# Moving the last two-operand GpSimd steps to VectorE and building a 32x32 inverse from blocks of 16 in a two-layer decoder trunk

## The chip, the cores and the metric

The kernel runs on one core of a Trainium2 chip. Its engines are TensorE (PE, matrix products, with its weight loads shown apart as PEld), VectorE (DVE), ScalarE (ACT), GpSimd (POOL) and SyncE (SP, which here issues every DMA). Each engine has a queue of its own and works it off in order. The metric is device microseconds for one execution; lower is better.

## What is computed

Two layers are applied to a sequence of 1024 tokens of width 1024, with a memory cross-attention beside each mixer and a SiLU gate on both. Layer 0 is latent attention with 12 heads, layer 1 a recurrent mixer with 24 heads of width 64:

```python
for i in range(DEPTH):                       # 0: attention, 1: recurrent
    h = rmsnorm(x, norm_g[i])
    u = h @ w_in[i]
    mix = mla_mixer(...) if i == 0 else rwkv7_mixer(...)
    y = concat([mix, memory_attention(...)]) * silu(gate)
    x = x + y @ w_out[i]
return rmsnorm(x, final_g)

def step(state, inp):                        # one token of rwkv7_scan, per head
    r_t, w_t, k_t, v_t, kk_t, a_t = inp
    sa = einsum('bhvk,bhk->bhv', state, -kk_t)
    state = (state * w_t[:, :, None, :] + sa[..., None] * (kk_t * a_t)[:, :, None, :]
             + v_t[..., None] * k_t[:, :, None, :])
    return state, einsum('bhvk,bhk->bhv', state, r_t)
```

All data are float32.

## The kernel before

**Precision and weights.** A float32 product is made of three TensorE products of halves: `split` writes a high part (ScalarE, fp32r) and a low part (a subtraction), and `mm3` (L162 to L164) multiplies high by high, low by high and high by low. `weights` (L142) loads weight tiles of 128x512 from DRAM (tile `wr`, four buffers), lets ScalarE write `wh` and a second engine the low part `wl` (four buffers each). In layer 1 that engine is VectorE (`self.lows`, set at L941). In layer 0 it is GpSimd, save for every second tile of the memory projections. `rope` (L516) multiplies one of its two products on GpSimd (L523), and `project` of the attention layer subtracts the low halves of the rotated queries there (L640, L641).

**Layer 1 in stages.** The 12 head pairs of the recurrent mixer and the two halves of the sequence (512 tokens each) make 24 items. Each item goes through five stages: `project`, `prep`, `invert`, `scan`, `norm`. In step s, item s is projected, item s-1 prepared, item s-2 inverted, and so on, so 28 steps cover all. Within a step the stages are generators, and `interleave` runs them in turns given by `ST = (4, 18, 13, 11, 11)`; between them lie parts of the output projections and of the memory heads. The framework takes that order as a priority and plans every engine's queue from it with costs of its own, so that instructions of all stages mix finely in each queue.

**The recurrence in chunks of 64 tokens.** An item has 8 chunks and 2 heads, so 16 systems of 64x64, unit triangular with a strictly triangular part N. `prep` computes them into `AM` (L1088, L1090), masked. The inverse of such a system is what `scan` multiplies with (`XT`, L1221). It is made of two 32x32 diagonal blocks and one block off the diagonal:

- End of `prep` (L1098 to L1110): the 32 diagonal blocks of 32x32 are written to DRAM (`sysd`, 16 DMAs), and ScalarE copies the off-diagonal parts into `A21`, the first 32 partitions of the tile `inv`.
- Start of `invert`: one DMA reads all blocks into `As`, each four times, one block per partition: partition = (block, column mod 4), free size 32x32. A constant is loaded into `U`.
- The loop of L1134 to L1143: back substitution, for u = 31 down to 1, one product and one sum on VectorE over u rows and up to 8 columns, 62 instructions per item.
- L1147 to L1155: eight TensorE transposes in two groups, evicted by ScalarE, put the columns back into matrices (`Uc`, partitions 32 to 95 of `inv`).
- The tail: a VectorE transpose (`X1`, L1159), copies into `U2` and `XT` (L1161, L1168), a product with `A21` (L1174), ScalarE copies (`M1`, L1183), a second product (L1188) and the copies into `XT` (L1191).

**Scan.** For each of the 8 chunks: `c` (L1215, L1217), a masking product on VectorE (`gm`, L1219), the product with the inverse (L1221), a copy (`SAV`, L1222), the new state (L1224, L1236). Each chunk needs the state of the one before it. `XT` has two buffers, so an item may be inverted while the one before it is scanned.

Of the kernel before, what the change touches and what calls it, by code (L numbers as in the profile page):

```python
# [23 lines left out]
P = 128  # L24
# [47 lines left out]
class Build:  # L72
    def __init__(self, tc, A, st):
        self.tc, self.nc, self.A = tc, tc.nc, A
        self.n, self.lows = 0, False
# [66 lines left out]
    def weights(self, src, cols=1024, shared=False):  # L142

# [3 lines left out]
        for c in range(0, cols, T):  # L147
# [6 lines left out]
            sub = nc.vector.tensor_sub if self.lows or shared and len(res) % 2 else nc.gpsimd.tensor_sub  # L154
            sub(lo[:, :n], raw[:, :n], hi[:, :n].bitcast(F32))  # L155
# [107 lines left out]
    def mem_kv(self, l, ms):  # L263
# [3 lines left out]
        for h in range(4):  # L267
            if h % 2 == 0:
                mk.append(self.g([P, 2, 256], s="mk"))
            w = self.weights(A["wmk"][l, h], shared=True)  # L270
            ps = self.mmt()
            self.gemm(ps[:, :256], w, ms, 8)
            nc.scalar.copy(mk[-1][:, h % 2, :], ps[:, :256])
        for cb in range(2):
            ws = self.weights(A["wmv"][l, cb, 0], shared=True) + self.weights(A["wmv"][l, cb, 1], shared=True)
# [138 lines left out]
    def layer0(self, ahead):  # L414

        nc, A, tc = self.nc, self.A, self.tc
        with ExitStack() as st:
# [98 lines left out]
            def rope(q, hf):  # L516
# [6 lines left out]
                nc.gpsimd.tensor_mul(sw[:], sw[:], sin[:, sl])  # L523
# [84 lines left out]
            def project(h):  # L608
# [26 lines left out]
                for t in rot:  # L635
# [4 lines left out]
                    nc.gpsimd.tensor_sub(a[64:128, :], t[0:64, :], a[0:64, :].bitcast(F32))  # L640
                    nc.gpsimd.tensor_sub(b[0:64, :], t[64:128, :], b[64:128, :].bitcast(F32))  # L641
# [137 lines left out]
    def layer1(self, x1, first, second):  # L779

        nc, A, tc = self.nc, self.A, self.tc
        with ExitStack() as st:
# [19 lines left out]

            cen = tl([P, P], F32, "cen")
# [4 lines left out]
            for t in ARs + XTs + [U2]:  # L808
                nc.gpsimd.memset(t[:], 0.0)
# [3 lines left out]
            env = dict(rmask=rmask, cen=cen, am=am, ip=ip, a_tile=a_tile, b_tile=b_tile, c_tile=c_tile, y_tile=y_tile)  # L813
# [127 lines left out]
            self.lows = True  # L941
# [37 lines left out]
    def prep(self, d, env):  # L979
# [117 lines left out]

        sysd = self.dram.tile([2, 16, 32, 32], F32, tag=f"sys{p % 2}", name=self.name("sysd"))  # L1098
        inv = self.g([P, 16, 32], s="inv")
        A21 = inv[0:32]  # L1100
        for b in range(2):
            for i in range(4):
                src = AM[i][32 * b : 32 * b + 32, :, 0:128].rearrange("p c (h t) -> p c h t", h=2)
                dst = sysd[b, 4 * i : 4 * i + 4].rearrange("(c h) r t -> r c h t", h=2)
                for c in range(2):
                    nc.sync.dma_start(dst[:, c], src[:, c, :, 32 * b : 32 * b + 32])
# [3 lines left out]
        d.update(f=f, SAV=SAV, BKT=BKT, AM=AM, bonus=bonus, inv=inv, sysd=sysd)  # L1110

    def invert(self, d, env):

        XT, U2, inv, sysd = (d[x] for x in ("XT", "U2", "inv", "sysd"))
# [5 lines left out]
        As = ip.tile([P, 32, 32], F32, tag="As", name=self.name("As"))  # L1120
        nc.sync.dma_start(
            As[:].rearrange("p a b -> p (a b)"),
            sysd[:].rearrange("b s r t -> (b s) (r t)").unsqueeze(1).broadcast_to([32, 4, 1024]),
        )
        U = ip.tile([P, 32, 8], F32, tag="U", name=self.name("U"))
        tmp = ip.tile([P, 32, 8], F32, tag="tmp", name=self.name("tmp"))
        E = V
        if d["hf"] == 1:
            c0 = self.smp.tile([P, P], F32, tag="c0", bufs=2, name=self.name("c0"))
            nc.sync.dma_start(c0[:], self.carry[d["p"]][:])  # L1130
            ACT.activation(c0[:], c0[:], AF.Copy, scale=d["f"][:, 8:9])
            d["c0"] = c0[:]
        nc.sync.dma_start(U[:].rearrange("p a b -> p (a b)"), self.A["cst"][:, CU : CU + 256])
        for u in range(31, 0, -1):  # L1134
            if u % 4 == 0:
                yield
            i0 = u // 4
            n = 8 - i0
            E.tensor_tensor(  # L1139
# [239 lines left out]
```

## Time and profile before

| what | us |
|---|---|
| median of 3 runs | 2541.62 (2540.92 to 2550.03) |
| profiled execution, own time | 2544.33 |
| profiled execution, span of the core | 2542.6 |

The page gives busy time by engine and by group of instructions; a group is named by its line, its engine, the tile written and the tiles read, with its shape, count, busy time and mean duration of one in ns. The chain of work that ended last goes back from the last instruction to what released each step. Matmuls overlap and their ends are modelled, so the duration of a matmul is longer than the time it holds the engine; the distance between two starts is what it costs. Layer 0 lasts to about 1080 us of the span, the pipelined steps of layer 1 to about 2445 us, and the rest is the end of the last output projection and the final norm.

### The profile page before, as it was taken

What the parts mean: (1) busy time and instruction counts of PE and PEld (TensorE: products, weight loads), DVE (VectorE), ACT (ScalarE), POOL (GpSimd) and SP (SyncE); (2) the same over time, 40 slices, a digit from 0 to 9 for tenths busy, and PEclk for the clock granted to TensorE, in tenths of its full rate; (3) what the DMA queues carried; (4) which work ended last, traced back from release to release, by engine and by line L of the source; (5) the groups of instructions that cost most, each with busy time, mean ns of one, the idle gap of its engine ahead of it and who ended that gap; (6) DMA issues with size and microseconds to landing.
All of it is one profiled execution on the core that took longest, in us unless ns stands there. A gap on an engine that the chain in (4) does not pass through costs nothing.

```text
span 2542.6 us, 39928 instructions
## 1 busy us (share of the span) xinstructions
PE 2434.1 (96%) x13298; PEld 2003.9 (79%) x13298; DVE 1883.6 (74%) x5564; ACT 1371.9 (54%) x2971; POOL 285.0 (11%) x344
## 2 busy tenths in 40 slices
PE   7899999999999999999999999999999999999997
PEld 5688777888888787878777777877787777788885
DVE  6655433677777647679888888788888888786986
ACT  5444335555445434556566665666666665654542
POOL 3332222322222240000000000000000000000000
PEclk8899999999999999999999999999999999999998
DMA  4242222111111345331222222322222223232341
GB/s 155 88 157 96 91 83 80 50 50 60 55 54 56 135 140 178 122 106 61 80 67 70 74 83 82 120 76 76 69 78 74 75 80 102 92 105 97 115 141 69
DMA packets 165983, 231.46 MB, mean 91 GB/s; under 512 B 46096, under 2 KB 67984, under 8 KB 165776
## 3 DMA queue, kind: packets, MB, share of 16 engines
q1 hardware_dynamic: 165776, 228.90, 27.5%
q8 instruction: 105, 1.72, 0.3%
q14 instruction: 102, 0.84, 0.1%
HBM read 187.66 MB, written 37.49 MB: 89 GB/s over the span
## 4 chain that ended last, share of the span: by engine, by line
PE 69%; DVE 16%; ACT 6%; issue 3%; DMA 2%; SPq 0%; DVEq 0%; POOL 0%; ACTq 0%; POOLq 0%
PE mm L162 14%; PE mm L163 13%; PE mm L164 13%; PE a L1088 3%; DVE tmp L1139 2%; PE c L1221 2%; PE pt L726 2%; DVE U L1143 2%; PE c L1224 1%; PE po L162 1%; PE y L1228 1%; PE po L163 1%; DVE wl L155 1%; PE y L1227 1%; PE po L164 1%
## 5 line engine op out<-in xcount | busy, mean ns | idle before, releaser
L153 ACT CAST wh<-wr 128x512 fp32r<-128x512 f32 (+3 forms) x500 | 298.6, 599 | 461.6 <-PE mm L163 363.0
L162 PE MATMUL mm<-xnh,wh 128*128 128x512 f32 x912 | 374.1, 411 | 0.8 <-DVE qml L134 0.6
L163 PE MATMUL mm<-xnl,wh 128*128 128x512 f32 x912 | 371.4, 407 | 0.0
L164 PE MATMUL mm<-xnh,wl 128*128 128x512 f32 x912 | 369.8, 406 | 0.0
L155 DVE TENSOR_TENSOR wl<-wr,wh 128x512 fp32r<-128x512 f32 (+2 forms) x352 | 237.2, 676 | 98.7 <-ACT wh L153 79.8
L155 POOL TENSOR_TENSOR wl<-wr,wh 128x512 fp32r<-128x512 f32 (+1 forms) x148 | 186.3, 1263 | 579.4 <-ACT wh L153 446.0
L162 PE MATMUL mm<-yh,wh 128*128 128x512 f32 x492 | 199.8, 406 | 5.5 <-DVE xr L391 5.3
L164 PE MATMUL mm<-yh,wl 128*128 128x512 f32 x492 | 197.6, 402 | 0.0
L162 PEld LDWEIGHTS mm<-xnh,wh 128*128 128x128 f32 x912 | 172.2, 189 | 30.4 <-issue 2.6
L163 PE MATMUL mm<-yl,wh 128*128 128x512 f32 x492 | 196.1, 399 | 0.0
L163 PEld LDWEIGHTS mm<-xnl,wh 128*128 128x128 f32 x912 | 172.4, 189 | 27.2 <-issue 1.4
L164 PEld LDWEIGHTS mm<-xnh,wl 128*128 128x128 f32 x912 | 172.2, 189 | 27.2 <-issue 1.0
L1069 POOL MEMSET SAV<- 64x512 f32 x48 | 24.9, 524 | 1385.6 <-DVE m L1261 250.7
L162 PE MATMUL mm<-xh,wh 128*128 128x512 f32 x416 | 168.9, 406 | 7.2 <-ACT xh L440 7.2
L163 PE MATMUL mm<-xl,wh 128*128 128x512 f32 x416 | 168.6, 405 | 2.9 <-DVE xl L441 2.9
L164 PE MATMUL mm<-xh,wl 128*128 128x512 f32 x416 | 168.1, 404 | 0.0
L1139 DVE TENSOR_TENSOR tmp<-As,U 128x60 f32<-128x60 f32 (+24 forms) x744 | 156.8, 211 | 13.2 <-DMA U<-in_cst_dram 1.1
L1143 DVE TENSOR_TENSOR U<-U,tmp 128x60 f32<-128x60 f32 (+24 forms) x744 | 157.2, 211 | 11.9
L1235 ACT ACTIVATE sc<-S,f 128x128 f32<-128x128 f32 x168 | 67.4, 401 | 170.0 <-DVE S L1236 155.5
L304 ACT ACTIVATE p<-b,sm 128x512 f32<-128x512 f32 (+2 forms) x144 | 82.9, 579 | 117.2 <-DVE sm L301 78.0
L391 DVE TENSOR_TENSOR xr<-mm,xr 128x512 f32<-128x512 f32 x123 | 84.5, 689 | 77.7 <-PE mm L164 77.2
L162 PEld LDWEIGHTS mm<-yh,wh 128*128 128x128 f32 x492 | 93.1, 189 | 24.3 <-DVE xr L391 3.5
(362 smaller groups left out, 6214.3 us busy)
## 6 DMA issues: line engine op xcount, KB each, us to landing
wr<-in_wu_dram SPq DMA_DIRECT2D x292, 256.0 KB, 2.6
wr<-in_wo_dram SPq DMA_DIRECT2D x122, 256.0 KB, 2.6
yr<-y SPq DMA_DIRECT2D x60, 256.0 KB, 3.7
As<-sysd SPq DMA_DIRECT2D x24, 512.0 KB, 4.3
y<-y SPq DMA_DIRECT2D x32, 256.0 KB, 2.0
y<-sg SPq DMA_DIRECT2D x32, 256.0 KB, 2.0
g<-u SPq DMA_DIRECT2D x24, 256.0 KB, 2.4
gt<-g SPq DMA_DIRECT2D x24, 256.0 KB, 2.8
```

Source lines behind the costliest of these rows:

```text
L153: nc.scalar.copy(hi[:, :n], raw[:, :n])
L155: sub(lo[:, :n], raw[:, :n], hi[:, :n].bitcast(F32))
L162: mm(ps, a[0], b[0], start=start, stop=False)
L163: mm(ps, a[0], b[1], start=False, stop=False)
L164: mm(ps, a[1], b[0], start=False, stop=stop)
L304: nc.scalar.activation(p[:, :own], ps[:, :own], AF.Exp, bias=sm[:, 0:1], accum_out=sm[:, 2 + i : 3 + i])
L391: nc.vector.tensor_add(xs[m][:], ps[:], xs[m][:])
L726: nc.tensor.transpose(pt[:, o : o + P], src, self.ident)
L1088: mm(ps[:, j * 256 : j * 256 + 256], BK[c // 4][:, c % 4, :], AR[:, c, :], start=True, stop=True)
L1139: E.tensor_tensor(out=tmp[:, 0:u, 0:n], in0=As[:, 0:u, u : u + 1].broadcast_to([P, u, n]), in1=U[:, u : u + 1, i0:8].broadcast_to([P, u, n ...
L1143: E.tensor_tensor(out=U[:, 0:u, i0:8], in0=U[:, 0:u, i0:8], in1=tmp[:, 0:u, 0:n], op=ALU.add)
L1235: ACT.activation(sc[:], cur, AF.Copy, scale=fc)
```

## The change

The change has two parts.

**GpSimd to VectorE.** `weights` always subtracts on VectorE; the product in `rope` and the two subtractions of the rotated queries move to VectorE. GpSimd keeps its memsets.

**The inverse from blocks of 16.** `prep` writes each 64x64 system whole (8 DMAs) and no longer fills `A21`. `invert` reads the four 16x16 diagonal blocks of each of the 16 systems, each twice, into `As` (8 DMAs of 16 partitions; partition = (column half, block, system)), and `A21` by a DMA. The substitution runs over u = 15 down to 1 with 8 columns each, so 30 instructions. ScalarE makes a transposed copy `UT`. Both go to DRAM (`Wd`, `WT`) and come back in three arrangements: `W1T` and `W2` as factors, and straight into the diagonal places of `inv`, now one zeroed tile for all items. The off-diagonal 16x16 blocks N12 are read from `sysd`. Two groups of four TensorE products make the missing block: first all products of eight systems at once, masked to their diagonal blocks by VectorE (`Tb`, with a constant `blk`), then the product with `W2`. ScalarE copies the result (`Ws`), and it goes through DRAM (`Wx`) into `inv`. From `X1` on nothing changes.

```diff
-    def weights(self, src, cols=1024, shared=False):
+    def weights(self, src, cols=1024):
...
-            sub = nc.vector.tensor_sub if self.lows or shared and len(res) % 2 else nc.gpsimd.tensor_sub
-            sub(lo[:, :n], raw[:, :n], hi[:, :n].bitcast(F32))
+            nc.vector.tensor_sub(lo[:, :n], raw[:, :n], hi[:, :n].bitcast(F32))
...
-                nc.gpsimd.tensor_mul(sw[:], sw[:], sin[:, sl])
+                nc.vector.tensor_mul(sw[:], sw[:], sin[:, sl])
...
-                    nc.gpsimd.tensor_sub(a[64:128, :], t[0:64, :], a[0:64, :].bitcast(F32))
-                    nc.gpsimd.tensor_sub(b[0:64, :], t[64:128, :], b[64:128, :].bitcast(F32))
+                    nc.vector.tensor_sub(a[64:128, :], t[0:64, :], a[0:64, :].bitcast(F32))
+                    nc.vector.tensor_sub(b[0:64, :], t[64:128, :], b[64:128, :].bitcast(F32))
...
+        sysd = self.dram.tile([16, 64, 64], F32, tag=f"sys{p % 2}", name=self.name("sysd"))
         for i in range(4):
-            src = AM[i][0:32, :, 0:128].rearrange("p c (h t) -> p c h t", h=2)
-            ACT.copy(A21[:, 4 * i : 4 * i + 4, :].rearrange("p (c h) t -> p c h t", h=2), src[:, :, :, 32:64])
+            for c in range(2):
+                dst = sysd[4 * i + 2 * c : 4 * i + 2 * c + 2].rearrange("h r t -> r h t")
+                nc.sync.dma_start(dst, AM[i][0:64, c, 0:128].rearrange("p (h t) -> p h t", h=2))
...
+        As = ip.tile([P, 16, 16], F32, tag="As", name=self.name("As"))
+        for half in range(2):
+            for i in range(4):
+                q = half * 64 + i % 2 * 32 + i // 2 * 16
+                nc.sync.dma_start(As[q : q + 16], sysd[:, 16 * i : 16 * i + 16, 16 * i : 16 * i + 16])
+        nc.sync.dma_start(A21, sysd[:, 0:32, 32:64].rearrange("s r t -> r s t"))
...
+        for u in range(15, 0, -1):
+            if u % 2 == 0:
+                yield
+            V.tensor_tensor(
+                out=tmp[:, 0:u], in0=As[:, 0:u, u : u + 1].broadcast_to([P, u, 8]),
+                in1=U[:, u : u + 1, :].broadcast_to([P, u, 8]), op=ALU.mult,
             )
+            V.tensor_tensor(out=U[:, 0:u], in0=U[:, 0:u], in1=tmp[:, 0:u], op=ALU.add)
+
+        UT = ip.tile([P, 8, 16], F32, tag="UT", name=self.name("UT"))
+        ACT.copy(UT[:].rearrange("p n r -> p r n"), U[:])
+        dt = lambda shape, n: self.dram.tile(shape, F32, tag=f"{n}{p % 2}", name=self.name(n))
+        Wd, WT, Wx = dt([2, 32, 16, 16], "Wd"), dt([32, 16, 16], "WT"), dt([32, 16, 16], "Wx")
+        for half in range(2):
+            cs = slice(8 * half, 8 * half + 8)
+            nc.sync.dma_start(Wd[:].rearrange("a q r n -> (a q) r n")[:, :, cs], U[64 * half : 64 * half + 64])
+            nc.sync.dma_start(WT[:, cs, :], UT[64 * half : 64 * half + 32])
         yield
+        W1T = self.g([16, 32, 16], s="W1T")
+        nc.sync.dma_start(W1T[:], WT[:].rearrange("q k m -> k q m"))
+        N12 = self.g([16, 32, 16], s="N12")
+        for j in range(2):
+            nc.sync.dma_start(
+                N12[:, 16 * j : 16 * j + 16, :],
+                sysd[:, 32 * j : 32 * j + 16, 32 * j + 16 : 32 * j + 32].rearrange("s k n -> k s n"),
+            )
+        W2 = ip.tile([P, 4, 16], F32, tag="W2", name=self.name("W2"))
+        nc.sync.dma_start(W2[:], Wd[1].rearrange("(g e) k n -> (e k) g n", e=8))
+        for par in range(2):
+            for j in range(2):
+                r0, c0 = 32 + 32 * j + 16 * par, 16 * par
+                nc.sync.dma_start(
+                    inv[r0 : r0 + 16, :, c0 : c0 + 16], Wd[par, 16 * j : 16 * j + 16].rearrange("s r n -> r s n")
+                )
+        yield
+
+        ps = b_tile()
+        for g in range(4):
+            mm(
+                ps[:, g * P : g * P + P], N12[:, 8 * g : 8 * g + 8, :].rearrange("p q n -> p (q n)"),
+                W1T[:, 8 * g : 8 * g + 8, :].rearrange("p q m -> p (q m)"), start=True, stop=True,
+            )
+        Tb = self.g([P, 4, P], s="Tb")
+        V.tensor_tensor(
+            out=Tb[:], in0=ps[:].rearrange("p (g f) -> p g f", f=P),
+            in1=env["blk"].unsqueeze(1).broadcast_to([P, 4, P]), op=ALU.mult,
+        )
+        yield
+        ps = b_tile()
+        for g in range(4):
+            mm(ps[:, g * 16 : g * 16 + 16], Tb[:, g, :], W2[:, g, :], start=True, stop=True)
+        Ws = ip.tile([P, 4, 16], F32, tag="Ws", name=self.name("Ws"))
+        ACT.copy(Ws[:].rearrange("p g n -> p (g n)"), ps[:, 0:64])
+        nc.sync.dma_start(Wx[:].rearrange("(g e) m n -> (e m) g n", e=8), Ws[:])
+        for j in range(2):
+            nc.sync.dma_start(
+                inv[32 + 32 * j : 48 + 32 * j, :, 16:32], Wx[16 * j : 16 * j + 16].rearrange("s r n -> r s n")
+            )
         Uc = [inv[32:64], inv[64:96]]
-        for ih in range(2):
-            yield
-            ps = b_tile()
-            for i in range(4):
-                nc.tensor.transpose(ps[0:32, i * P : i * P + P], U[:, :, ih * 4 + i], self.ident)
-            for b in range(2):
-                src = ps[0:32, :].rearrange("p (i s c) -> p i s c", i=4, c=4)[:, :, b * 16 : b * 16 + 16, :]
-                dst = Uc[b][:, :, ih * 16 : ih * 16 + 16].rearrange("p s (i c) -> p i s c", c=4)
-                ACT.copy(dst, src)
```

More of the change, by code (lines that the diff above doesn't have):

```diff
@@ L269, in mem_kv @@
                 mk.append(self.g([P, 2, 256], s="mk"))
-            w = self.weights(A["wmk"][l, h], shared=True)
+            w = self.weights(A["wmk"][l, h])
             ps = self.mmt()
@@ L274, in mem_kv @@
         for cb in range(2):
-            ws = self.weights(A["wmv"][l, cb, 0], shared=True) + self.weights(A["wmv"][l, cb, 1], shared=True)
+            ws = self.weights(A["wmv"][l, cb, 0]) + self.weights(A["wmv"][l, cb, 1])
             ps = self.mmt()
@@ L801, in layer1 @@
             prev = tl([P, 37], F32, "prev")
+            blk = tl([P, P], F32, "blk")
+            nc.sync.dma_start(blk[:], A["cst"][:, CU + P : CU + 256])
+            inv = tl([96, 16, 32], F32, "inv")
             cen = tl([P, P], F32, "cen")
@@ L807, in layer1 @@
             U2 = tl([P, 4, P], F32, "U2")
-            for t in ARs + XTs + [U2]:
+            for t in ARs + XTs + [U2, inv]:
                 nc.gpsimd.memset(t[:], 0.0)
@@ L812, in layer1 @@
             am = self.cst[:, CAM : CAM + 256]
[L813 removed]
+            env = dict(rmask=rmask, cen=cen, inv=inv, blk=blk[:], am=am, ip=ip, a_tile=a_tile, b_tile=b_tile, c_tile=c_tile, y_tile=y_tile)
             xns, twa = [None, None], [tl([P, T], F32R, f"twa{i}") for i in range(2)]
@@ L1095, in prep @@
         yield
-        sysd = self.dram.tile([2, 16, 32, 32], F32, tag=f"sys{p % 2}", name=self.name("sysd"))
-        inv = self.g([P, 16, 32], s="inv")
-        A21 = inv[0:32]
-        for b in range(2):
-            for i in range(4):
[L1103 to L1106, printed above, removed]
+        sysd = self.dram.tile([16, 64, 64], F32, tag=f"sys{p % 2}", name=self.name("sysd"))
         for i in range(4):
-            src = AM[i][0:32, :, 0:128].rearrange("p c (h t) -> p c h t", h=2)
-            ACT.copy(A21[:, 4 * i : 4 * i + 4, :].rearrange("p (c h) t -> p c h t", h=2), src[:, :, :, 32:64])
-        d.update(f=f, SAV=SAV, BKT=BKT, AM=AM, bonus=bonus, inv=inv, sysd=sysd)
+            for c in range(2):
+                dst = sysd[4 * i + 2 * c : 4 * i + 2 * c + 2].rearrange("h r t -> r h t")
+                nc.sync.dma_start(dst, AM[i][0:64, c, 0:128].rearrange("p (h t) -> p h t", h=2))
+        d.update(f=f, SAV=SAV, BKT=BKT, AM=AM, bonus=bonus, sysd=sysd)
     def invert(self, d, env):
-        XT, U2, inv, sysd = (d[x] for x in ("XT", "U2", "inv", "sysd"))
+        XT, U2, sysd, p = (d[x] for x in ("XT", "U2", "sysd", "p"))
+        inv = env["inv"]
         A21 = inv[0:32]
@@ L1131, in invert @@
             ACT.activation(c0[:], c0[:], AF.Copy, scale=d["f"][:, 8:9])
             d["c0"] = c0[:]
-        nc.sync.dma_start(U[:].rearrange("p a b -> p (a b)"), self.A["cst"][:, CU : CU + 256])
-        for u in range(31, 0, -1):
-            if u % 4 == 0:
+        nc.sync.dma_start(U[:].rearrange("p a b -> p (a b)"), self.A["cst"][:, CU : CU + P])
+        for u in range(15, 0, -1):
+            if u % 2 == 0:
                 yield
-            i0 = u // 4
-            n = 8 - i0
-            E.tensor_tensor(
-                out=tmp[:, 0:u, 0:n], in0=As[:, 0:u, u : u + 1].broadcast_to([P, u, n]),
-                in1=U[:, u : u + 1, i0:8].broadcast_to([P, u, n]), op=ALU.mult,
-            )
-            E.tensor_tensor(out=U[:, 0:u, i0:8], in0=U[:, 0:u, i0:8], in1=tmp[:, 0:u, 0:n], op=ALU.add)
```

24 lines of the change are left out of this document (8 added, 16 removed).

## The prediction

> **What bounds the kernel now.** I read the page first: busy time, the chain of work that ended last, and the costliest groups.
>
> ```profile
> span 2542.6 us, 39928 instructions
> ...
> PE 2434.1 (96%) x13298; PEld 2003.9 (79%) x13298; DVE 1883.6 (74%) x5564; ACT 1371.9 (54%) x2971; POOL 285.0 (11%) x344
> ...
> PE 69%; DVE 16%; ACT 6%; issue 3%; DMA 2%; SPq 0%; DVEq 0%; POOL 0%; ACTq 0%; POOLq 0%
> ...
> L1139 DVE TENSOR_TENSOR tmp<-As,U 128x60 f32<-128x60 f32 (+24 forms) x744 | 156.8, 211 | 13.2 <-DMA U<-in_cst_dram 1.1
> L1143 DVE TENSOR_TENSOR U<-U,tmp 128x60 f32<-128x60 f32 (+24 forms) x744 | 157.2, 211 | 11.9
> ...
> L1235 ACT ACTIVATE sc<-S,f 128x128 f32<-128x128 f32 x168 | 67.4, 401 | 170.0 <-DVE S L1236 155.5
> ```
>
> TensorE is busy nearly all the time and holds 69% of the chain; VectorE has 16%; GpSimd is hardly on it. So time can only come from what TensorE waits for, or from its own work. The view by windows splits that over the layers. Its columns are the stretch, its length, the busy time of PE, PEld, DVE, ACT and POOL with instruction counts, the granted clock, the DMA share and GB/s.
>
> ```profile
> 0.00:1080.00 1080.00, 1031.23 (x5561) 865.09 (x5562) 662.39 (x1388) 508.78 (x1074) 262.19 (x300) 0.99 0.29 97
> 1080.00:2445.00 1365.00, 1323.88 (x7350) 1076.69 (x7349) 1158.89 (x4024) 830.85 (x1824) 22.85 (x44) 1.00 0.27 87
> ...
> 0.00:100.00 100.00, 76.86 (x303) 59.77 (x304) 69.58 (x120) 48.39 (x84) 37.22 (x31) 0.91 0.38 127
> 100.00:200.00 100.00, 91.57 (x556) 81.49 (x555) 51.89 (x90) 43.43 (x81) 30.09 (x22) 0.95 0.44 144
> ...
> 1100.00:1200.00 100.00, 97.20 (x524) 77.58 (x523) 89.28 (x325) 66.19 (x142) 2.16 (x4) 1.00 0.22 69
> ...
> 2300.00:2400.00 100.00, 97.00 (x520) 80.11 (x518) 78.07 (x226) 52.54 (x116) 1.04 (x2) 1.00 0.31 102
> ```
>
> In layer 0 TensorE is idle for 49 us, 32 of them in the first 200. In the steps of layer 1 it is idle for 41 us of 1365, while VectorE is 85% busy. VectorE is a second bound there, but a weak one: the last two rows are the first and the last of 13 windows of 100 us, and they hold the same PE time at 89 and at 78 us of VectorE. A straight line through all 13 gives 0.09 us of PE for each us of VectorE.
>
> **The change, part by part.** *VectorE in layer 1.* The old loop takes (156.8 + 157.2) / 24 = 13.1 us per item. The new one has 30 instructions, two each of 8, 16, ... 120 elements. By shape:
>
> ```profile
> L1139 DVE TENSOR_TENSOR tmp<-As,U 128x76 f32<-128x76 f32 x24 | 5.6, 234 | 0.3
> ...
> L1139 DVE TENSOR_TENSOR tmp<-As,U 128x8 f32<-128x8 f32 x24 | 3.9, 162 | 0.4
> ...
> L1090 DVE TENSOR_TENSOR AM<-a,cst 128x512 f32<-128x512 f32 x96 | 65.4, 683 | 1.8 <-PE a L1088 0.8 <-PE y L1227 0.4
> ```
>
> That is 162 ns at 8 elements and 234 at 76, about 1.06 ns for each more; the mean shape, 64, comes to 221 ns, and 30 of them to 6.6 us. `Tb` adds one instruction like L1090, 0.68 us. VectorE sheds 13.1 - 6.6 - 0.7 = 5.8 us per item, 139 us in all, 10 points of its share. By the line through the windows that gives TensorE 0.09 x 139 = 12 us back. Its ends are 0 (the two windows quoted) and 41 us (all idle time); I take 12. ScalarE loses eight small copies and gains two no longer than L1235's 0.40 us: nothing, for it is 61% busy.
>
> *TensorE in layer 1.* Eight transposes go; two groups of four float32 products come, each of two passes. The timeline gives what such groups hold, from start to next start:
>
> ```profile
> 1365.36 0.60 PE L1151 MATMUL b<-cst,U 128*32 128x128 f32 x4
> 1365.80 0.39 PE L1221 MATMUL c<-gm,XT 128*128 128x128 f32 x2
> ...
> 1369.70 1.12 PE L1174 MATMUL b<-X,inv 32*128 32x128 f32 x8 [0.54 <-DVE X L1159]
> 1370.75 0.50 PE L164 MATMUL mm<-xnh,wl 128*128 128x512 f32 x1
> ...
> 1377.85 0.95 PE L1006 MATMUL a<-cst,sq 128*128 128x2 f32 x8
> 1378.66 0.48 PE L163 MATMUL mm<-xnl,wh 128*128 128x512 f32 x1
> ```
>
> Gone: two groups of 0.44 us, 0.88. Added: one like L1174 (few rows, 128 columns both ways), 1.05 us, and one like L1006 (few columns behind full weights), 0.81. Net +1.0 us per item, +24 us. Of this nothing is hidden as long as TensorE is the bound; if it falls into idle time, that is the 12 us above.
>
> *The inverse as a chain.* Its place in one step:
>
> ```profile
> 1365.05 0.17 DVE L1143 TENSOR_TENSOR U<-U,tmp 128x8 f32<-128x8 f32 x1
> ...
> 1368.85 0.70 DVE L1159 STREAM_TRANSPOSE X<-inv 32x512 f32<-32x512 f32 x1 [1.29 <-ACT inv L1155]
> ...
> 1372.34 0.21 DVE L1139 TENSOR_TENSOR tmp<-As,U 128x31 f32<-128x31 f32 x1
> ...
> 1407.71 0.17 DVE L1143 TENSOR_TENSOR U<-U,tmp 128x8 f32<-128x8 f32 x1
> ```
>
> The loop is spread over 35.5 us, since other work has its turns between; from its end to `X1` it takes 3.6 us. The DMAs of the new chain are not in the trace; the nearest are these (KB, us to landing; then SP's own time to issue 11; then DMA share and GB/s while only such writes ran, and while weights did):
>
> ```profile
> As<-sysd SPq DMA_DIRECT2D x24, 512.0 KB, 4.3
> ...
> sysd<-AM SPq DMA_DIRECT2D x384, 8.0 KB, 1.5
> ```
>
> ```profile
> 1306.89 5.84 SPq L1106 DMA_DIRECT2D sysd<-AM  x11
> ```
>
> ```profile
> 1309.00:1311.00 2.00, 2.00 (x15) 1.75 (x14) 1.89 (x9) 0.40 (x1) 0.00 (x0) 1.00 0.08 12
> ...
> 1319.00:1321.00 2.00, 1.93 (x11) 1.30 (x9) 0.70 (x2) 1.76 (x7) 0.00 (x0) 1.00 0.79 270
> ```
>
> New, from the loop's end to `X1`: `UT` 0.4; four issues 2.1; a landing 1.5; eight issues 4.2; a landing 1.5; products, `Tb`, products 2.5; `Ws` 0.4; issue and landing 2.0; two issues and a landing 2.6. Sum 17.2 us, 13.6 more than now. The loop before it ends earlier by 6.5 us (its own work alone) to 17.5 (in proportion over its 35.5). So `X1` comes between 7 us later and 4 earlier. What hides it is that `scan` of the item starts a step later, and a step lasts 1365 / 28 = 49 us. I take nothing; if the cover is gone, the second rival gives the price.
>
> SP issues 33 DMAs per item for 18, 15 x 0.53 = 8 us more in a step; it mostly waits for free weight buffers, so nothing. But it works in order: `Wd` waits there for the loop and `Wx` for `Ws`, and the next weights are queued behind them. What follows on ScalarE (`wh`), VectorE (`wl`) and then TensorE is covered by the four `wr` and four `wl` buffers.
>
> Packets: some 8,100 more per item, of 32 to 256 bytes. In the first of the two windows 24 KB in packets of 128 bytes took 0.08 x 16 x 2 = 2.6 us of engine time, 14 ns a packet; in the second, packets of 2 KB took 96 ns. At 14 ns each of 16 engines is busy 7 us more per step, 14 points onto 27%; at 96 ns it would be 49 us, the whole step. I take 14, the row of like size, and so nothing.
>
> On this the Trainium skill speaks against the change: "DMA: Bandwidth & Descriptors", "Rules for kernel authors", has small transfers coalesced, since under 64 KB one pays mostly overhead. The landings agree (1.5 us for 8 KB); no run here yet shows 32-byte rows.
>
> *Layer 0.* VectorE gets 118 subtractions of 512 columns, 30 narrower ones, 14 products and 24 subtractions: 156 x 0.69 + 15 = 122 us. It also loses a hindrance:
>
> ```profile
> L155 DVE TENSOR_TENSOR wl<-wr,wh 128x512 fp32r<-128x512 f32 x262 | 179.5, 687 | 54.9 <-ACT wh L153 36.4 <-PE b L1151 9.8 <-PE c L1224 3.0
> ```
>
> ```profile
> 561.01 1.29 POOL L640 TENSOR_TENSOR qsa<-rt,qsa 64x512 fp32r<-64x512 f32 x1 [2.06 <-DVE sm L307]
> ...
> 561.18 1.34 DVE L309 TENSOR_SCALAR p<-p,sm 128x384 f32<-128x384 f32 x1
> ```
>
> The first row is the subtraction without GpSimd beside it, in layer 1. In the others a scaling on VectorE lasts exactly until GpSimd's subtraction ends. So VectorE goes from 61% to at most 73% of layer 0, under the share that it has in layer 1. TensorE there stands still only in the first 200 us: 32 us is the most to win, and a few us can be lost where low parts queue behind the norms. I take -2.
>
> Sum: +24 - 12 - 2 = +10 us on the profiled execution, whose own time is 2544.3 (span 2542.6). The median of the runs is 2.7 lower, 2541.6, and I add to that: 2552.
>
> **The rivals.** *Faster: VectorE was the real second bound.* For it: 16% of the chain, the loop on it, and the locks of layer 0. Against: the weak slope. Then all 41 us of idle time go, 24 come, and a third of the 32 us at the start: 2541.6 - 17 - 10 = 2515.
>
> *Slower: TensorE waits for a hop through DRAM.* Its queue is in order, and the plan puts the new products where it expects their operands. For it: three landings in series that the old chain did not have, and weights behind them on SP. Against: the loads of `As` make nobody on TensorE wait now. If one landing per item is late by the distance between the two landing rows (4.3 - 1.5 = 2.8), less the 0.5 us that TensorE waits there today, it costs 24 x 2.3 = 55 us: 2607. Above 0.1 us per item (12.7 us less the 10 of the sum, over 24) it decides between no change and slower.
>
> **How the numbers follow.** A measurement of this kernel tells 0.5% (12.7 us) from no change. My forecast, 2538 to 2566, has 0.42: no change 0.29, slower 0.13. The faster rival has 0.30 (faster 0.27, no change 0.03), the slower one 0.28 (slower 0.26, no change 0.02). Together: faster 0.27, same 0.34, slower 0.39. The range reaches to both rivals, 2512 to 2608.
>
> **What would show it.** In the changed profile: the loop at 6.6 us per item; VectorE near 75% in the steps; PE idle there at about 30 us; the added groups at 1.9 us per item. Wrong would be: waits of PE for `N12`, `W1T`, `inv` or `Tb` above 1 us per item, `wh` waiting for DMA, SP's time per issue above 1 us, or a DMA share above 0.5.

## The result: 3.7% slower, and the profile after

The changed kernel takes 2636.9 us (median of 4), the kernel before 2541.3 beside it on the same chip: 1.037 times as long, 95% interval 1.035 to 1.040. The forecast was 2552 with a range to 2608.

The page of the changed kernel, as quoted of the kernel before (busy time, chain of waits, DMA packets):

```profile
span 2633.9 us, 40050 instructions
...
PE 2507.9 (95%) x13490; PEld 2064.7 (78%) x13490; DVE 1841.9 (70%) x5006; ACT 1334.4 (51%) x2829; POOL 55.7 (2%) x159
...
PE 80%; DVE 9%; ACT 7%; issue 2%; DMA 2%; SPq 0%; DVEq 0%; ACTq 0%
...
DMA packets 366957, 233.11 MB, mean 89 GB/s; under 512 B 248480, under 2 KB 272032, under 8 KB 366752
```

TensorE is still 95% busy, as if only its work had grown. The windows from the first to the last product with `XT` show that this is not so (columns as in the forecast; the first row is the kernel before, the second the changed one):

```profile
1139.70:2499.50 1359.80, 1318.89 (x7360) 1073.37 (x7360) 1146.33 (x3964) 817.50 (x1799) 21.73 (x42) 1.00 0.27 86
```

```profile
1114.20:2591.70 1477.50, 1402.80 (x7541) 1137.89 (x7541) 1056.44 (x3255) 778.30 (x1663) 21.94 (x42) 0.96 0.30 80
```

The first product with `XT` comes 25.5 us earlier (1114.2 against 1139.7), so layer 0 has gained. The steps of layer 1 then lose 117.7 us: TensorE idles 74.7 us in place of 40.9 (+33.8) and is busy 83.9 us longer. Its granted clock is 0.96 in place of 1.00; 4% of 1402.8 is 56 us, an estimate. It leaves 28 us for the added products. (The run with shared tiles below has the same products at a clock of 1.00, and there they add 30: 1349.13 against 1318.89.) So about a third of the loss is idle time that the profile shows as such, and about half is a slower clock that it shows as busy time.

Both come from one place, the tail of the inverse. The timeline of TensorE in one step:

```profile
1218.90 0.39 PE L162 MATMUL mm<-xnh,wl 128*128 128x512 f32 x1
1221.36 1.84 PE L1206 MATMUL b<-X,inv 32*128 32x128 f32 x8 [2.07 <-DVE X L1191]
1224.35 1.91 PE L1220 MATMUL b<-U,M 128*32 128x128 f32 x8 [1.15 <-ACT M L1215]
1227.09 0.80 PE L1253 MATMUL c<-gm,XT 128*128 128x128 f32 x2 [0.82 <-ACT XT L1223]
...
1231.72 0.63 PE L161 MATMUL mm<-xnl,wh 128*128 128x512 f32 x1
...
1282.83 1.91 PE L1220 MATMUL b<-U,M 128*32 128x128 f32 x8 [1.15 <-ACT M L1215]
```

TensorE waits for `X1`, then for `M1`, then for `XT`, with no projection to do between. Afterwards a product takes 0.63 us where it took 0.39, and the product with A21 1.84 where the kernel before had 1.12. From L1220 to the next L1220 it is 58.5 us; before, such a step took 48. Windows of one microsecond show the clock:

```profile
1219.00:1220.00 1.00, 0.29 (x2) 0.00 (x0) 0.20 (x1) 0.62 (x1) 0.00 (x0) 1.00 0.35 32
...
1222.00:1223.00 1.00, 1.00 (x6) 0.90 (x5) 0.94 (x4) 0.00 (x0) 0.00 (x0) 0.50 0.03 2
...
1234.00:1235.00 1.00, 1.00 (x4) 0.81 (x3) 1.00 (x4) 0.16 (x1) 0.00 (x0) 0.50 0.00 0
...
1236.00:1237.00 1.00, 1.00 (x6) 0.80 (x5) 1.00 (x8) 0.47 (x1) 0.00 (x0) 1.00 0.00 0
```

Just after 2.07 us of idle time the clock halves, and it stays halved for 13 us.

Why had TensorE nothing to do? ScalarE's timeline, one step later:

```profile
1277.41 0.62 ACT L152 CAST wh<-wr 128x512 fp32r<-128x512 f32 x1 [2.14 <-PE mm L161]
1281.71 1.06 ACT L1215 COPY M<-b 32x128 f32<-32x128 f32 x4 [3.68 <-PE b L1206]
1282.79 1.28 ACT L998 ACT_TABLE_LOAD   x1
1284.09 0.69 ACT L998 ACTIVATE sig<-a,prm 128x512 f32<-128x512 f32 x1
...
1286.12 0.62 ACT L1292 ACTIVATE ys<-yT 128x512 f32<-128x512 f32 x1
1286.64 0.59 ACT L865 ACTIVATE sg<-mm 128x512 f32<-128x512 f32 x1
```

ScalarE stands still for 3.68 us and then does `M1` of the inverse, and directly behind it `sig` of `prep`, `ys` of `norm` and `sg` of the gate: three stages of the next step. The product that `sig` reads had ended at 1267.9, 16 us before. All of them write fresh tiles of the heap. From this came the theory that decided, after two others had fallen.

### The profile page after: what moved, and what is told of

It reads as the page before. It is cut to its first block, busy times and chain, and to the rows that moved or that the text cites. A ratio compares the mean times of both kernels' runs of the same rounds, so it can differ in the third digit from the quotient of the medians.

```text
span 2633.9 us, 40050 instructions
## 1 busy us (share of the span) xinstructions
PE 2507.9 (95%) x13490; PEld 2064.7 (78%) x13490; DVE 1841.9 (70%) x5006; ACT 1334.4 (51%) x2829; POOL 55.7 (2%) x159
## 2 busy tenths in 40 slices
DMA packets 366957, 233.11 MB, mean 89 GB/s; under 512 B 248480, under 2 KB 272032, under 8 KB 366752
## 4 chain that ended last, share of the span: by engine, by line
PE 80%; DVE 9%; ACT 7%; issue 2%; DMA 2%; SPq 0%; DVEq 0%; ACTq 0%
PE mm L160 17%; PE mm L161 16%; PE mm L162 16%; PE a L1088 3%; PE c L1256 2%; PE c L1253 2%; PE pt L724 2%; PE c L1247 1%; PE y L1260 1%; PE y L1259 1%; PE po L160 1%; PE po L161 1%; PE c L1249 1%; PE po L162 1%; PE a L1006 1%
## 5 line engine op out<-in xcount | busy, mean ns | idle before, releaser
L153 DVE TENSOR_TENSOR wl<-wr,wh 128x512 fp32r<-128x512 f32 (+3 forms) x500 | 329.6, 661 | 195.7 <-ACT wh L152 175.8
L160 PE MATMUL mm<-xnh,wh 128*128 128x512 f32 x912 | 383.7, 422 | 4.3 <-DVE u L830 4.0
L162 PE MATMUL mm<-xnh,wl 128*128 128x512 f32 x912 | 376.4, 413 | 0.0
L1254 DVE COPY SAV<-c 64x128 f32<-64x128 f32 x192 | 53.8, 280 | 87.2 <-PE c L1253 85.9
L297 DVE TENSOR_REDUCE sm<-b 128x1 f32<-128x256 f32 (+1 forms) x176 | 90.2, 527 | 24.7 <-PE b L686 10.1
L162 PEld LDWEIGHTS mm<-yh,wl 128*128 128x128 f32 x492 | 92.6, 188 | 17.9 <-issue 0.4
L161 PEld LDWEIGHTS mm<-yl,wh 128*128 128x128 f32 x492 | 92.9, 189 | 16.6 <-DVE yl L129 0.7
```

What stands on the lines that cost most here:

```text
L153: nc.vector.tensor_sub(lo[:, :n], raw[:, :n], hi[:, :n].bitcast(F32))
L160: mm(ps, a[0], b[0], start=start, stop=False)
L161: mm(ps, a[0], b[1], start=False, stop=False)
L162: mm(ps, a[1], b[0], start=False, stop=stop)
L297: nc.vector.tensor_reduce(sm[:, i : i + 1], ps[:, :own], AX.X, ALU.max, negate=True)
L1254: V.tensor_copy(SAV[i][0:64, j, :], pa[0:64, :P])
```

## The experiments

In the table, *light step* is the median distance, over the second to the fifth step of the inverse, from the second product of the tail (L1220) of one item to that of the next; in these steps no output projection fills TensorE. Ratios are to the kernel before on the same chip. The labels are those of the expectations below.

| run | us | ratio (95%) | light step, us |
|---|---|---|---|
| before | 2541 to 2545 | | 48.1 |
| changed | 2636.9 | 1.037 (1.035 to 1.040) | 58.0 |
| part one alone (e1) | 2516.7 | 0.989 (0.987 to 0.991) | 47.9 |
| part two alone (e2) | 2668.7 | 1.050 (1.047 to 1.052) | 58.0 |
| A21 in its own tile (e3) | 2647.9 | 1.041 (1.038 to 1.043) | 58.3 |
| DMAs by GpSimd (e4) | 2664.5 | 1.047 (1.044 to 1.051) | 57.1 |
| unread products (e5) | 2660.1 | 1.045 (1.040 to 1.050) | 57.2 |
| loop in 3 turns (e6) | 2630.0 | 1.033 (1.029 to 1.037) | 56.6 |
| last hop not awaited (e7) | 2547.8 | 1.001 (0.999 to 1.002) | 50.9 |
| tiles shared (e9) | 2538.2 | 0.997 (0.996 to 0.998) | 49.7 |
| tiles only claimed early (e17) | 2542.3 | 0.998 (0.997 to 1.000) | 49.8 |
| old inverse and a hop (e18) | 2566.9 | 1.008 (1.005 to 1.011) | 51.0 |
| the same, claimed early (e20) | 2533.0 | 0.996 (0.994 to 0.997) | 47.6 |
| old inverse, claimed early (e21) | 2514.4 | 0.989 (0.987 to 0.990) | 47.4 |

### The two parts add up

> Part one alone: GpSimd's subtractions and products go to VectorE, the inverse stays as it was. In the profile of the changed kernel the first product of the first scan with XT starts 25 to 31 us earlier than before (1114 against 1140 us; the first write of sysd 1048.5 against 1080.3), while the steps of layer 1 take 118 us longer. If the early gain belongs to part one, this kernel takes 2541 - 30 = 2511 us and its layer 1 is as long as before (1360 us from the first to the last product with XT). If instead the early gain came from the new plan that the other part brings, it takes 2541, give or take 12.

> Part two alone: the inverse from blocks of 16, with GpSimd's steps left where they were. If the parts add up, 2637 + 30 = 2667 us, with TensorE's clock granted at about 0.96 in layer 1 as in the changed kernel. If the loss in layer 1 needed part one as well (the low parts of the weights are on VectorE there in both kernels, so nothing suggests it), 2560 or less.

Measured 2516.7 and 2668.7: part one gains 28 us, part two costs 123, together +95, and the change has +96. Everything in layer 1 belongs to part two.

### Is it SP's queue or the packets?

```diff
-        A21 = inv[0:32]
+        A21 = self.g([32, 16, 32], s="A21")
```

> The changed kernel, but A21 has a tile of its own from the rotating heap in place of the first 32 partitions of the one inv tile, so that its load no longer waits on SP until the product with A21 of the item before has read it. Queue theory: weights stand behind that load on SP and TensorE has no projection to do in the inverse's tail; with the wait gone over half of the 96 us loss returns, below 2590, and the waits of TensorE for X1, M1 and XT shrink. Place theory: X1 is late because of the chain of hops itself, so 2615 to 2640 and the waits for X1, M1 and XT stay near 33 us.

In every DMA of `invert` but the load of `c0`:

```diff
-        nc.sync.dma_start(...)
+        nc.gpsimd.dma_start(...)
```

> The changed kernel, but all DMAs of the inverse (the reads of As and A21, the constant, Wd, WT, W1T, N12, W2, Wx and the writes into inv) are issued by GpSimd, which is 2% busy, so that SP keeps the weights, sysd and the carries. Queue theory: weights no longer stand behind waits for U or Ws, and over half of the 96 us loss returns, below 2590. Place theory: the hops are as long as before and TensorE still reaches the products of the tail too early: 2610 to 2650. If an issue by GpSimd takes longer than SP's 0.45 us, the chain gets longer and the time goes above 2650.

Both are slower than the changed kernel, at 2647.9 and 2664.5, and the light steps stay at 57 to 58 us. The first is 8 us above what place theory allowed. The second is where the expectation puts a longer chain: GpSimd takes 0.56 us to issue a load of `As` (SP: 0.45), and such a load lands after 2.8 us in place of 1.9. The weights are not what is missing: queue theory falls. In the second run GpSimd's queue also needs far fewer packets for the same transfers:

```profile
DMA packets 175342, 233.12 MB, mean 88 GB/s; under 512 B 51872, under 2 KB 77728, under 8 KB 175136
```

191,615 packets less bring nothing back. Since the chain got longer at the same time, this run alone does not settle the packets; the kernel with shared tiles below does, for it moves the 366,957 packets of the changed kernel and takes 99 us less. The Trainium skill, "DMA: Bandwidth & Descriptors", "Rules for kernel authors", would have small transfers coalesced, since under 64 KB one pays mostly overhead. The landings agree (1.9 us for 16 KB of `As`, 2.7 us for 256 KB of weights), but the shared kernel issues as many transfers as the changed one, so their number was not what cost.

### What the clock does, and what a hop is worth

```diff
         ps = b_tile()
+        for _ in range(8):
+            mm(ps[:], d["twa"][0][:, 0:P], d["twa"][0][:], start=True, stop=True)
         for g4 in range(4):
```

and likewise 5 and 4 into `c_tile()` behind the two products of the tail.

> The changed kernel with 17 more products of 128x512 per item that nobody reads: 8 ahead of the product with A21 (into the tile that it then overwrites), 5 behind it and 4 behind the second product of the tail (into scan's c tile). One takes 0.23 us from start to start. In the changed kernel TensorE stands idle there for 2.07, 1.15 and 0.8 to 1.5 us, and its granted clock then is 0.50 for 5 to 14 us. If the idle time takes the clock down, the clock in layer 1 rises from 0.96 to 0.99 or more and about 57 us of lower clock go; the products cost nothing where TensorE waited and up to 3.9 us in the 11 or so steps where it did not (43 us), so 2600 to 2640 us. If the clock falls for another reason, it stays near 0.96 and the products add 40 to 94 us: 2680 to 2730.

```diff
-            if u % 2 == 0:
+            if u % 4 == 0:
                 yield
```

> The changed kernel with one number changed: the substitution loop gives way to other stages at every fourth u in place of every second, 3 turns in place of 7, so that everything behind it is planned four of 13 turns earlier in the step, some 15 us. Nothing else is changed: the same instructions, the same DMAs. Place theory (the tail stands at the end of the step, and the scan that opens the next step needs its result at once): X1 and XT are in time, the waits for X1, M1 and XT fall from 33 us to a few and the granted clock of layer 1 is 0.99 or more; 2637 less 80 to 100, so 2535 to 2560. If the loss came from the added work, the packets or the issues on SP as such, the time stays above 2600.

```diff
-                inv[...], Wx[16 * j : 16 * j + 16].rearrange("s r n -> r s n")
+                inv[...], sysd[:, 16:32, 0:16].rearrange("s r n -> r s n")
```

> The changed kernel, but the off-diagonal 16x16 places of inv are filled from sysd, which has been in DRAM for a step, in place of Wx; Ws is still made and written to Wx, but nobody waits for it, so the result of the inverse is left wrong. It takes the last of the three round trips through DRAM out of the chain and nothing else (landing of inv from Wx 2.1 us, of Wx 1.8, the issues between). Place theory: X1 can start some 5 us earlier, and most of the waits go: 2560 to 2600. If one hop more or less does not decide, above 2620.

The window over the steps of the run with unread products, from the first to the last product with `XT`:

```profile
1115.00:2610.00 1495.00, 1452.99 (x7912) 1172.45 (x7913) 1058.14 (x3252) 775.98 (x1662) 22.02 (x42) 0.99 0.31 79
```

The clock is back at 0.99, so the idle time was what took it down. The time is not back: 2660, 20 us above the expected range. TensorE is busy 50 us longer than in the changed kernel (1452.99 against 1402.80), though the better clock gives back some 42 (3% of 1402.8). So the 408 products cost some 92 us by this estimate, nearly the full 94 of 408 times 0.23, and not the 43 at most that had been expected. Giving TensorE something to do is no cure where the step itself is too long.

Without the last round trip 89 us return (2636.9 to 2547.8), 12 more than the best that was expected: the chain of hops sets the length of the step. (This kernel leaves out the off-diagonal 16x16 blocks of the inverse: entries of the system stand in their places.)

The early loop is the miss that told most. The loop did end sooner, in 17 us in place of 30, and the waits for the tail went, as the list of TensorE's waits shows (us in all, times, longest), the changed kernel first:

```profile
PE b L1206 <- DVE X L1191: 12.2, 10, 2.1
PE c L1253 <- ACT XT L1223: 10.9, 9, 1.6
PE b L1220 <- ACT M L1215: 10.4, 10, 1.2
```

```profile
PE c L1253 <- DVE gm L1251: 10.6, 28, 1.0
```

In their place are waits within the scan, this one the longest, and the light step is 56.6 us. This speaks against place theory, that the tail's result is simply due at the end of the step: with the tail in time, something else is too late by nearly as much. It is not proof by itself, for the early loop costs some 30 us even in kernels without the fault, as two runs below show.

One of them looks back at the old inverse with fewer turns (every eighth `u` on top of part one alone); it was expected at 2517, give or take 12, and gave 2547.7 us, 31 above part one alone. This was not explained; fewer turns cost about 30 us in the shared kernel below as well.

### Who may claim a buffer

Claim theory says this: a tile of the heap (54 buffers) is claimed where it is first written, and the planner lets tiles be claimed only in the order in which the program writes them. That is what the order on ScalarE suggested: `M1` is the last tile of a step's program, `sig` the first of the next. So the next step would wait for the whole chain of hops.

```diff
+        t1, t2 = self.g(s="t1"), self.g(s="t2")
+        W1T = t1[0:16].rearrange("p (q m) -> p q m", m=16)
+        N12 = t2[0:16].rearrange("p (q n) -> p q n", n=16)
...
+        Tb = t2[:].rearrange("p (g f) -> p g f", f=P)
...
+        X1 = t1[0:32].rearrange("p (a b) -> p a b", b=32)
...
+        M1 = Tb[:, :, 0:32]
```

> The changed kernel with the same instructions, but the five heap tiles of the inverse are two: W1T and X1 share one, N12, Tb and M1 the other, both claimed when W1T is. Claim theory: buffers of the heap are claimed in the order in which the program is written, so in the changed kernel no tile of the next step (sig and a of prep, ys of norm, sg of the gate, u of the projection) can be claimed until the tail has come to M1; in the trace ScalarE does nothing between 1278.1 and 1281.7 but wait for the tail and then does M1, sig, ys and sg at once. With the claims ahead of the hops, the other stages run while the hops are under way: the light steps fall from 58 us to 48 to 51, the clock of layer 1 is 0.99 or more, and the time is 2530 to 2560. Place theory (the tail's result is late for scan, whatever else may run): the hops are as long as before, so 2610 to 2640.

It takes 2538.2 us, 99 less than the changed kernel, with the same instructions. TensorE and ScalarE around the tail of a light step, and the window of the steps:

```profile
1261.29 0.39 PE L161 MATMUL mm<-xnl,wh 128*128 128x512 f32 x1
1261.83 1.12 PE L1207 MATMUL b<-t,inv 32*128 32x128 f32 x8 [0.15 <-DVE t L1192]
1262.89 0.50 PE L162 MATMUL mm<-xnh,wl 128*128 128x512 f32 x1
```

```profile
1254.93 0.60 ACT L865 ACTIVATE sg<-mm 128x512 f32<-128x512 f32 x1
...
1262.99 1.06 ACT L1216 COPY t<-b 32x128 f32<-32x128 f32 x4 [1.33 <-PE b L1207]
```

```profile
1119.80:2496.80 1377.00, 1349.13 (x7514) 1095.43 (x7514) 1055.48 (x3238) 775.21 (x1658) 21.79 (x42) 1.00 0.34 86
```

`sg` of the next step now runs 8 us ahead of `M1` (here `t`), projections stand on both sides of the product with A21, its wait is 0.15 us in place of 2.07, and the clock is 1.00. The hops are as many as before. Is it the order of the claims, or that two buffers do for five?

> The kernel with shared tiles, with 53 heap buffers in place of 54. It tells whether the order of the claims or the number of free buffers is what counts. Claim theory: as with 54, within 15 us. If the heap is simply full and the sharing helps by freeing buffers, taking one away gives back a good part of what the sharing brought: 20 us or more above the run with 54.

2549.5 us, 11 above: with one buffer fewer still within what claim theory allows. The cleaner test changes the claims alone:

```diff
+        for t in (Tb, X1, M1):
+            G.memset(t[:, 0:1, 0:1], 0.0)
```

with the five tiles named together where `W1T` is.

> The changed kernel, with five separate heap tiles as there, but GpSimd writes one element of each partition of Tb, X1 and M1 when W1T is read back, so that these are claimed then and not behind their hops. Nothing is shared, and more buffers are held than in the changed kernel, not fewer. Claim theory: near the shared kernel's 2538 us, 2530 to 2565, with light steps near 50 us. If the shared kernel was faster because it needs fewer buffers, this one is no better than the changed kernel: 2620 or more.

2542.3 us, light steps 49.8. ScalarE now does `sig` 15 us ahead of `M1`, where it stood directly behind it:

```profile
1249.27 0.69 ACT L998 ACTIVATE sig<-a,prm 128x512 f32<-128x512 f32 x1
...
1264.20 1.06 ACT L1214 COPY M<-b 32x128 f32<-32x128 f32 x4 [1.35 <-PE b L1206]
```

Three small writes on an idle engine, which compute nothing and hold buffers longer, bring 95 of the 96 us back. The order of the claims is shown to be the cause.

> The kernel with shared tiles, and its loop gives way at every fourth u in place of every second (3 turns in place of 7), as in the earlier run with separate tiles, which took 2630 us. Claim theory: there the earlier loop did not help because Tb, X1 and M1 were still claimed behind their hops and now held up AM of the item after; with the claims out of the way the time is within 20 us of the shared kernel with 7 turns. If the early loop is bad by itself, 2580 or more.

2568.6 us: the early loop costs 30 even so, more than claim theory said and less than the bound set for the other case. Sharing does bring 61 us to it (2630.0 to 2568.6). That `Tb` there held up `AM` of the item after was argued, not shown.

### One hop in the old inverse

```diff
+        hx = self.dram.tile([64, 16, 32], F32, ...)
+        nc.sync.dma_start(hx[:], inv[32:96])
+        nc.sync.dma_start(inv[32:96], hx[:])
```

> Part one alone with the old inverse, plus one round trip through DRAM that it does not need: the two diagonal blocks in inv are written out and read back to the same place before X1. It prices a hop in a kernel whose tail has no other. Two issues and two landings make about 5 us. Claim theory: X1 and M1 are claimed behind the hop, so the step gets longer by it wherever the output projection does not fill it, in some 13 light steps: 2517 + 40 to 65, so 2555 to 2585 us. If a scan that starts a step later hides a hop, as the forecast had it, 2517 to 2530.

> The same needless round trip in the old inverse whose X1 and M1 share one tile claimed at the start (2517 us without the round trip). Claim theory: the same hop, but the next step's tiles are claimed without it, so most of it is hidden: 2517 to 2535. If a hop costs by the lateness of XT itself, as much as with the separate tiles: 2555 to 2585.

The two transfers of the hop, 128 KB each, land after 2.2 and 2.6 us. The hop costs 50 us (2566.9), as claim theory had it. The second run missed: 2562.6, only 4 less. Its shared tile, named at the start, is first written by `X1`, and so behind the hop; it did not do what it was to do. With one column written at the start:

```diff
         t1 = self.g(s="t1")
+        nc.gpsimd.memset(t1[:, 0:1], 0.0)
```

> The old inverse with the needless round trip and the shared tile, and GpSimd writes the tile's first column when the inverse starts. In the run before, the shared tile was first written by X1, so behind the round trip: a tile is claimed where it is first written, not where it is named, and the next step's tiles still stood behind the hop (M1's claim alone was gone, and 4 of 50 us with it). Here the claim is made ahead of the hop. Claim theory: most of the 50 us goes, 2517 to 2540. If it stays above 2555, a hop in the old tail costs by the lateness of XT and the claims do not matter there.

> The same without the round trip: part one alone, the old inverse, X1 and M1 in one tile that is claimed when the inverse starts. Light steps already run at 48 us with TensorE 97% busy, so claim theory gives 2505 to 2520, at best 10 us below part one alone; a held buffer that others need would show as 2530 or more.

2533.0 us: the same hop costs 19 us over its counterpart (2514.4) in place of 50. The light step is 47.6 us, against 47.4 without it; where the other 19 are lost was not followed up. Without the hop the early claim is worth 2 us, within the intervals, since the old chain fits into the step. (Sharing one tile between `X1` and `M1` without the early write, expected at 2500 to 2520, gave 2516.5.)

### Where layer 0 gained

The kernel before, with `weights` alone changed to VectorE:

> The kernel before, with only the low parts of the weights (weights in layer 0) moved to VectorE; rope's product and the rotated queries stay on GpSimd. Part one as a whole brought 28 us, and 20 of them are already there at 200 us of the span, ahead of any head of the attention. If the weights' low parts were what TensorE waited for in the opening, this kernel keeps at least three quarters of it: 2517 to 2525 us. If the gain came from the rope and the queries, whose subtractions lock VectorE, 2535 to 2545.

2524.2 us, ratio 0.991 (0.990 to 0.993): 21 of part one's 28 us come with the low parts of the weights. The costs of the same subtraction, on GpSimd in the kernel before and on VectorE in part one alone, and the windows of part one alone:

```profile
L155 POOL TENSOR_TENSOR wl<-wr,wh 128x512 fp32r<-128x512 f32 x118 | 158.5, 1349 | 399.5 <-ACT wh L153 345.8 <-PE mm L164 19.5 <-PE b L690 8.5
```

```profile
L154 DVE TENSOR_TENSOR wl<-wr,wh 128x512 fp32r<-128x512 f32 x452 | 309.0, 685 | 121.4 <-ACT wh L153 102.7 <-PE b L1149 9.5 <-PE c L1215 3.0
```

```profile
0.00:100.00 100.00, 90.23 (x395) 71.19 (x396) 75.06 (x162) 57.43 (x98) 0.71 (x6) 1.00 0.47 148
100.00:200.00 100.00, 91.65 (x575) 81.70 (x574) 59.90 (x122) 43.60 (x81) 0.00 (x0) 0.98 0.46 148
```

In the first 100 us TensorE is 13.4 us busier than before (90.23 against 76.86), with its clock at 1.00 in place of 0.91, and by 200 us it has issued 970 products in place of 859. The low part takes VectorE half as long as GpSimd (685 against 1349 ns). That is the factor of two that the Trainium skill gives for two-input operations on GpSimd ("GPSIMD Engine Reference", "4.1 Engine selection"); the rows agree.

But TensorE did not wait for low parts. Its waits in the first 100 us of the kernel before, which are all that its list has there, are for the norm on VectorE (`sqa`, its sum of squares, and `rw`) and for the halves of the input (`xh`, `xl`). The timeline shows what held `sqa` up:

```profile
PE b L208 <- DVE sqa L186: 8.7, 3, 3.4
PE mm L162 <- ACT xh L440: 7.2, 1, 7.2
PE b L220 <- DVE rw L213: 4.3, 2, 3.1
PE mm L163 <- DVE xl L441: 2.9, 4, 0.8
```

```profile
70.38 3.17 POOL L155 TENSOR_TENSOR wl<-wr,wh 128x512 fp32r<-128x512 f32 x2 [3.18 <-ACT wh L153]
...
72.34 1.75 DVE L186 TENSOR_TENSOR sqa<-sqa,sqb 128x512 f32<-128x512 f32 x1
...
74.62 0.68 DVE L186 TENSOR_TENSOR sqa<-sqa,sqb 128x512 f32<-128x512 f32 x1
```

The sum takes VectorE 1.75 us while GpSimd subtracts and 0.68 us afterwards. In the first 200 us, 22 of VectorE's 37 instructions of this kind (two operands, 128x512, float32) overlap with one of GpSimd's and take 1.22 us on average; the other 15 take 0.68. In part one alone none takes more than 0.70 us, the wait for `sqa` is gone, and those for `rw` and `xl` fall to 1.9 and 0.6 us. So what the traces show is that GpSimd's subtractions held VectorE up, and VectorE TensorE. No run parts this from the shorter time of the subtraction itself.

## Why the prediction failed, step by step

**What bounds the kernel** held: TensorE does, and VectorE is a weak second. The -12 us that the slope of 0.09 gave came out where the hops do not hurt: in the steps of the shared kernel VectorE has 91 us less than before and TensorE idles 27.9 us in place of 40.9. That is as much luck as reading, for through the 13 windows the two are but loosely tied (correlation -0.32), and no run shows that it was VectorE's lighter load that took the 13 us away.

**VectorE's part** was right. The loop was forecast at 6.6 us per item:

```profile
L1136 DVE TENSOR_TENSOR U<-U,tmp 128x120 f32<-128x120 f32 (+4 forms) x360 | 78.7, 219 | 5.7
L1132 DVE TENSOR_TENSOR tmp<-As,U 128x120 f32<-128x120 f32 (+4 forms) x360 | 78.6, 218 | 5.6
```

157.3 / 24 = 6.55. Its share of the steps is 72% and, where the hops do not hurt, 77%; 75 was forecast.

**TensorE's part** was nearly right: +24 us forecast, 30 in the shared kernel, whose clock is 1.00.

**The chain's length** was right; **its cover** is the step that failed. Forecast: 17.2 us from the loop's end to `X1`, compensated by a loop that ends 6.5 to 17.5 us earlier, so that `X1` comes between 7 us later and 4 earlier, and behind that "`scan` of the item starts a step later, and a step lasts 49 us. I take nothing". The loop and `X1` of one item (the third) stand so in the changed kernel and, below it, in the kernel before (VectorE; the rows of the loop give least, median and longest ns and the first and last start of an instruction):

```profile
L1132 DVE TENSOR_TENSOR tmp<-As,U x15: 159/223/284, 1170.4 to 1200.6; 128x120 f32<-128x120 f32 x1, 128x112 f32<-128x112 f32 x1, 128x104 f32<-128x104 f32 x1, 128x96 f32<-128x96 f32 x1
...
L1136 DVE TENSOR_TENSOR U<-U,tmp x15: 166/215/273, 1171.3 to 1200.8; 128x120 f32<-128x120 f32 x1, 128x112 f32<-128x112 f32 x1, 128x104 f32<-128x104 f32 x1, 128x96 f32<-128x96 f32 x1
```

```profile
1220.52 0.70 DVE L1191 STREAM_TRANSPOSE X<-inv 32x512 f32<-32x512 f32 x1
```

```profile
L1139 DVE TENSOR_TENSOR tmp<-As,U x31: 159/210/230, 1180.6 to 1221.1; 128x60 f32<-128x60 f32 x3, 128x28 f32<-128x28 f32 x2, 128x54 f32<-128x54 f32 x2, 128x48 f32<-128x48 f32 x2
```

```profile
1224.46 0.70 DVE L1159 STREAM_TRANSPOSE X<-inv 32x512 f32<-32x512 f32 x1 [1.40 <-ACT inv L1155]
```

The loop takes 30.6 us (1170.4 to 1201.0) where that of the same item took 40.9 (1180.6 to 1221.5). It ends 10 us earlier, within the range given; the 35.5 us of the forecast were those of a shorter one, four items on. From the loop's end to `X1` it is 19.5 us in place of 3.0, where 17.2 and 3.6 had been put. So `X1` comes 6 us later, as the forecast allowed: the sum was right, and what should have made it harmless was not there. There is no step of slack: the tail is the last thing of its step, `scan` opens the next with its result (L1253 waits for `XT`), and the other stages, which should have run meanwhile, could not claim their tiles before `M1`. Claimed ahead of the hops, with the hops as they are, the same kernel takes 95 us less. The trace of before held this, in ScalarE's timeline:

```profile
1226.47 1.06 ACT L1183 COPY M<-b 32x128 f32<-32x128 f32 x4 [1.01 <-PE b L1174]
1227.55 1.28 ACT L998 ACT_TABLE_LOAD   x1
1228.84 0.69 ACT L998 ACTIVATE sig<-a,prm 128x512 f32<-128x512 f32 x1
...
1230.76 0.62 ACT L1260 ACTIVATE ys<-yT 128x512 f32<-128x512 f32 x1
```

There, too, `sig` and `ys` stand directly behind `M1`; with 3.0 us from the loop's end to `X1` hardly anything waited for it.

**The second rival** named the place (TensorE's in-order queue, a hop through DRAM) and the sign, at 0.28. Its price, 2.3 us per item, was too low for three reasons: the waits add up over `X1`, `M1` and `XT`; the clock, which the forecast left out altogether, then costs more than the waits (an estimated 56 us against 34); and the rest of the step is held up too. Its remark that TensorE would wait for the hop because of its own order is only half of it, as the early claims showed: the hops stayed and the waits went.

**The queue and the packets** were right to be put at nothing: the run with A21 in its own tile and the shared kernel show it. The DMA share in the steps is 0.30; 41 points were forecast, from 27 and 14.

**Layer 0** had the wrong size: -2 forecast, -28 measured. The forecast named the hindrance, VectorE held up while GpSimd subtracts, but saw it only at the rotated queries in the middle of the layer (its two rows end at 562.30 and 562.52, so "exactly" is too much said) and gave it no price. It stood at the start, between the norm's sums and TensorE. "32 us is the most to win" was read from idle time in windows that also showed the clock at 0.91 and 0.95; about a third of the gain is clock (9% of 76.86 and 5% of 91.57 us, less the 2% of 91.65 that remain, make an estimated 10 us).

Put together, the forecast's own sum with layer 0 at -28 is 2526; the shared kernel, in which the cover exists, takes 2538. The missing cover is all but 12 us of what the forecast lacked.

## What to carry to other kernels

Before calling a longer chain hidden, find out what else may run while it lasts: look in the trace for the first instructions of the next stage, and whether they start as soon as their inputs are there or always directly behind the same unrelated instruction. In a planned kernel with a shared pool, a tile first written at the end of a chain of round trips makes every later tile wait; claim it ahead of the chain, by sharing a tile that is live anyway or by writing one element. And price an idle gap of TensorE with the clock that follows it.

The best version found is part one with the old inverse: 2516.7 us, or 2514.4 with the early claim, 0.989 (0.987 to 0.990) of the kernel before. The inverse from blocks of 16 does not pay even with its claims in order.

## What had not been expected of the hardware

A gap of 2.07 us on TensorE was enough to halve its granted clock, and it stayed at 0.50 for 13 us, the last six of them without a gap above 0.1 us. (In the 8 us before it there is no other gap above 0.1 us.) The longest gap in the steps of the kernel before leaves it at 1.00 (TensorE's timeline, then the window around it):

```profile
1665.35 1.12 PE L1042 MATMUL a<-rk,cst 128*128 128x512 f32 x2 [1.37 <-DVE rk L1024]
```

```profile
1650.00:1700.00 50.00, 46.27 (x262) 37.31 (x261) 42.97 (x153) 33.47 (x71) 0.00 (x0) 1.00 0.24 76
```

Shorter gaps close together did the same: in the changed kernel, gaps of 1.22 and 0.45 us from 1686.6 and 1688.6 on took the clock from 1.00 (1688 to 1689) to 0.50 (1690 to 1691). So the length of a single gap does not decide.

The Trainium skill, "TensorE: Matmul & The Clock Gate", "HAM oscillation — how this bites in real kernels", names gaps above about 3.4 us as the ones to avoid. The halving agrees, the length does not, and the measurement decides: in this kernel two microseconds are too many.
